# Reading out the sample states of a decoder step: one column moving past each state instead of the state moving past eight columns

## The chip, the core and the metric

The program runs on one core of a Trainium2 chip. A core has five engines that run at the same time and meet at semaphores: PE (TensorE, matmuls into PSUM), DVE (VectorE), ACT (ScalarE), POOL (GpSimd) and SP (SyncE, which here only issues DMAs). The metric is the device time of one execution in microseconds (us), lower is better.

## The reference

One inference step of a two-layer decoder for a prompt of 256 tokens and 8 samples of one token each. Both share all weights and run side by side as 264 columns. Layer 1 (the "odd" layer) has a Mamba-2 mixer with 32 heads of 64 channels in 4 groups, and a state of 128 numbers for each channel. For the samples its recurrence is one step from a given state:

```
    cb = jnp.einsum('bctgn,bcsgn->bctsg', cm, bm)
    dx = dt[..., None] * x
    y_diag = jnp.einsum('bctsgr,bcsgrp->bctgrp', cb[..., None] * decay, dx)
...
    states = jnp.einsum('bcsgn,bcsgrp->bcgrpn', bm, dstate[..., None] * dx)
...
        return dec[..., None, None] * carry + st, carry
```

For one token this is: new state = decay x old state + B (dt x), which is an output too (`s_ssd`), and y = C . new state, summed over the 128 state numbers n. Then y is gated, normalised and goes through the output projection. Everything is fp32.

## The kernel before

The odd mixer (`odd_mixer`) is one long loop over 41 tiles of the input projection (`k.linear(41, 8, "wio", ...)`): PE does the matmuls of tile m, then `use(m, p)` takes the result out, and from m = 9 on `slot(m - 9)` adds a slot's worth of other work behind it. The order on each engine is the order in which the code is written (`manual_schedule`); an engine never overtakes its own earlier instruction. Weight tiles come by DMA, issued by SP: some are used as they are (`wl`, line 128, plain fp32: two passes over 264 columns for a matmul), others come as `wr` and are split into `wh` by ACT (line 51) and `wl` by DVE or POOL (line 55), and then take three passes (lines 110 to 112).

The sample states are 32 units (g, b): 4 groups of 8 samples. A unit is a tile S of 128 state numbers (partitions) by 512 channels. `samples(want)` stands first in a slot (the "S" of `ORDER`), right behind the matmuls of the projection tile, and moves a few units on: `read` of those updated in an earlier slot, `update` (a matmul, line 1464, and a DVE pass, line 1465), `state_in` (DMA into one of 6 buffers S) and `decay` (POOL). `read(g, b, S)` issues the DMA that writes S out and multiplies it with C. In this kernel the small matrix `Cd[:, g, b*8:(b+1)*8]` (128 by 8, zero but for column b, made once by POOL at m = 10) is the stationary operand and S moves past it as 512 columns; the 8 units of a group add up in one PSUM tile `pys` (8 samples by 512 channels). The pool of `pys` has one buffer (one PSUM bank), so the next group's first write waits for whoever reads the last group's. Behind the eighth unit ACT copies `pys` to an SBUF tile `sd` (line 1477); the next call of `samples` first runs `turn_back` (line 1480): four PE transposes of `sd`, which bring channels back to the partitions, and a DVE copy into `ys`. So in three slots PE has four transposes between the projection tile and the next group's first read; the fourth `turn_back` has no read behind it.

In ACT's queue a slot begins with what `use` writes: `zt` twice (Tanh and copy of the projection tile, lines 1562 and 1563), then `act_queue` (waiting exponentials and SiLUs: lines 1365 to 1368 and 1313); the split of the next weight tile (line 51) stands ahead of these, since `linear` prepares weights while it issues the matmuls.

Of the kernel before, what the change touches and what calls it, by code (L numbers as in the profile page):

```python
# [7 lines left out]
F32 = mybir.dt.float32  # L8
# [4 lines left out]
AF = mybir.ActivationFunctionType  # L13
# [5 lines left out]
T = 264  # L19
NP = 256  # L20
NS = 8
# [1148 lines left out]
def odd_mixer(k, xh, xl, norm, mixed):  # L1170

    tc, nc, ins, outs = k.tc, k.nc, k.ins, k.outs
    V = nc.vector
    Act = nc.scalar.activation
    with ExitStack() as es:
        pool = es.enter_context(tc.tile_pool(name="od", bufs=1))
# [3 lines left out]
        gen = lambda: pg.tile([128, 512], F32, name="pgen")  # L1180
# [17 lines left out]
        xbc = pool.tile([128, 24, T], F32, name="xbc")  # L1198
# [9 lines left out]
        Bn = pool.tile([128, 2, 4, 128], F32, name="Bn")  # L1208
        cb = pool.tile([128, 2, 4, 128], F32, name="cb")
        sqa = pool.tile([128, T], F32, name="sqa")  # L1210
        Cd = pool.tile([128, 4, NS * NS], F32, name="Cd")
        ys = pool.tile([128, 16, NS], F32, name="ys")
        sqs = pool.tile([128, 16, NS], F32, name="sqs")
        ysw = pool.tile([128, 16, NS], F32, name="ysw")
# [180 lines left out]
        def sums(n):  # L1395
            s = st[n]
            py = gen()
            for i in range(2):
                R = slice(64 * i, 64 * i + 64)
                nc.tensor.matmul(py[R, 0:128], s["dx"][:, 0, R], s["seg"][:, i, 0], start=True, stop=True,  # L1400
                                 skip_group_check=True)
                nc.tensor.matmul(py[R, 128:256], s["dx"][:, 1, R], s["seg"][:, i, 1], start=True, stop=False,
                                 skip_group_check=True)
                nc.tensor.matmul(py[R, 128:256], s["St"][:, R], s["ea"][:, i], start=False, stop=True,
                                 skip_group_check=True)
            s["py"] = py

        def skip(n):
            y = xbc[:, n, 0:NP]
            V.scalar_tensor_tensor(y, y, dsk[:, 0, n:n + 1], st[n]["py"][:, 0:NP], op0=ALU.mult, op1=ALU.add)  # L1410
# [31 lines left out]
        def sample_x(g):  # L1442
            p = gen()
            for i in range(4):
                nc.tensor.transpose(p[:NS, ts(i, 128)], xbc[:, 4 * g + i, NP:T], k.ident)
            sd = pool.tile([NS, 512], F32, name="sd")
            V.tensor_tensor(sd.rearrange("b (h p) -> b h p", h=8), p[:NS].rearrange("b (h p) -> b h p", h=8),
                            snat[:, 8 * g:8 * g + 8, None].to_broadcast([NS, 8, 64]), op=ALU.mult)
            h = sdx[g] = sdr[:, g % 2]
            Act(h[:NS], sd, AF.Copy)  # L1450
            V.tensor_sub(h[32:], sd, h[:NS])

        def state_in(g, b):
            S = pool.tile([128, 512], F32, name="S", bufs=6)
            nc.sync.dma_start(S, ins["ssd0"][:, b, ts(g, 512)])
            return S

        def decay(g, b, S):
            nc.gpsimd.tensor_tensor(S.rearrange("n (h p) -> n h p", h=8), S.rearrange("n (h p) -> n h p", h=8),
                                    bc[:, 2 + b, 8 * g:8 * g + 8, None].to_broadcast([128, 8, 64]), op=ALU.mult)  # L1460

        def update(g, b, S):
            p = gen()
            nc.tensor.matmul(p, sel(NS, b), sdx[g], start=True, stop=True)
            V.scalar_tensor_tensor(S, p, xbc[:, 16 + g, NP + b:NP + b + 1], S, op0=ALU.mult, op1=ALU.add)

        pys = []

        def read(g, b, S):
            nc.sync.dma_start(outs["s_ssd"][:, b, ts(g, 512)], S)  # L1470
            if b == 0:
                pys.append(p1.tile([128, 512], F32, name="pys"))
            nc.tensor.matmul(pys[-1][:NS], Cd[:, g, b * NS:(b + 1) * NS], S, start=b == 0, stop=b == NS - 1,
                             skip_group_check=True)
            if b == NS - 1:
                y = pool.tile([NS, 512], F32, name="sd")
                Act(y, pys[-1][:NS], AF.Copy)
                turned.append((g, y))

        def turn_back(g, y):  # L1480
            p = gen()
            for i in range(4):
                nc.tensor.transpose(p[:, ts(i, NS)], y[:, ts(i, 128)], k.ident[:NS, :NS])
            V.tensor_copy(ys[:, 4 * g:4 * g + 4], p[:, 0:4 * NS].rearrange("p (i t) -> p i t", i=4))

        U = [(g, b) for g in range(4) for b in range(NS)]
        Ss, turned = {}, []
        at = [0, 0, 0, 0]

        def samples(want):  # L1490


            while turned:
                turn_back(*turned.pop(0))
            while at[3] < at[2]:
                read(*U[at[3]], Ss.pop(U[at[3]]))
                at[3] += 1
                if turned:
                    break
            while at[2] < want:  # L1500
                g, b = U[at[2]]
                assert at[1] > at[2]
                if b == 5 and g < 3:
                    sample_x(g + 1)
                update(g, b, Ss[g, b])
                at[2] += 1
            while at[0] < len(U) and at[0] < at[3] + 6:
                Ss[U[at[0]]] = state_in(*U[at[0]])
                at[0] += 1
            while at[1] < at[0] and at[1] < at[2] + 3:  # L1510
                decay(*U[at[1]], Ss[U[at[1]]])
                at[1] += 1


        start = {s: n for n, s in enumerate(START)}
        head, left = [], set(range(16))

        def slot(s):
            if s == 6:
                V.tensor_scalar(sdr[0:32], k.ones[0:32, 0:1, None].to_broadcast([32, 2, 512]), 0.0, None, op0=ALU.mult)  # L1520
                sample_x(0)
            for o in ORDER:
                if o == "S" and s > 5:
                    samples(SAMPLES[s - 6] if s - 6 < len(SAMPLES) else len(U))
                if o == "U" and s - 4 in start:
                    sums(start[s - 4])
                if o == "T" and s - 2 in start:
                    states(start[s - 2])
                if o == "W" and s - 2 in start:
                    weights(start[s - 2])  # L1530
                if o == "R" and s in start:
                    turns(start[s])
                if o == "K" and s - 4 in start:
                    skip(start[s - 4])
                    left.remove(start[s - 4])
            if s == LAST:
                assert at[3] == len(U) and not turned
                V.tensor_tensor(sqs, xbc[:, 0:16, NP:T], dsk[:, 0, :, None].to_broadcast([128, 16, NS]), op=ALU.mult)
                V.tensor_add(ys, ys, sqs)
                V.tensor_tensor(ysw, ys, dsk[:, 1, :, None].to_broadcast([128, 16, NS]), op=ALU.mult)  # L1540
            n = s - 16
            if 0 <= n < 16:
                assert n not in left
                if s > LAST:
                    sample_gate(0 if s == LAST + 1 else 2 * s - 47, min(16, 2 * s - 45))
                gate(n)
                if n > 0:
                    gated(n - 1)
                if n == 15:
                    gated(n)  # L1550

        def use(m, p):
            if m == 0:
                head.append(softplus(p))
                next(head[0])
                V.tensor_scalar(cw, cw, 0.5, None, op0=ALU.mult)
                return
            if m < 25:
                conv(m + 15 if m < 9 else m - 9, p)
            else:  # L1560
                z = pool.tile([128, 2, T], F32, name="zt", bufs=2)
                Act(z[:, 0], p[:, 0:T], AF.Tanh, scale=0.5)
                Act(z[:, 1], p[:, 0:T], AF.Copy)
                act_queue()
                finish_silus()
                V.scalar_tensor_tensor(z[:, 0], z[:, 0], 1.0, z[:, 1], op0=ALU.add, op1=ALU.mult)
                V.tensor_copy(szs[:, m - 25], z[:, 0, NP:T])
                st[m - 25]["z"] = z[:, 0]
            next(head[0], None)
            if m == 10:  # L1570
                groups()
                V.tensor_scalar(dsk[:, 1], dsk[:, 1], 0.5, None, op0=ALU.mult)
                y_parts.extend(pool.tile([128, 16, T], F32R, name=nm) for nm in ("yh", "yl"))
                nc.gpsimd.memset(Cd, 0.0)
                nc.gpsimd.tensor_copy(Cd[:, :, 0:NS * NS:NS + 1], xbc[:, 20:24, NP:T])
            if m >= 9:
                slot(m - 9)

# [185 lines left out]
```

## Time and profile before

| | |
|---|---|
| median of 3 runs | 2337.83 us (2336.58 to 2338.54) |
| the profiled execution | 2338.07 us, its span 2336.4 us |
| PE busy in the span | 2157.9 us (92%) |
| DVE, ACT, POOL busy | 1657.3, 945.1, 1008.6 us |
| mean granted TensorE clock | 0.967 of full speed |
| reads of the sample states | from 1189.2 to 1327.6 us of the span |

The span is the time from the first to the last instruction; 1.7 us lie around it. The granted clock has two levels, 1.0 (2.4 GHz) and 0.5 (1.2 GHz); the mean is over the span. An fp32 matmul is two PE records (passes) and two weight loads (PEld). A PE record's length includes time in which the array already works on the next one, so the distance between starts is what a pass costs.

### The profile page before, as it was taken

How to read it: one execution, taken by the hardware profiler on the slowest of the kernel's cores; microseconds unless marked ns; L12 is line 12 of the kernel's file. 1: busy time of each engine (PE TensorE's matmuls, PEld its weight loads, DVE VectorE, ACT ScalarE, POOL GpSimd, SP SyncE). 2: the span in 40 equal slices, each digit the busy share in tenths (PEclk: the TensorE clock that was granted, in tenths of full speed). 3: DMA queues.
4: the chain of work that ended last, by engine and by line, in shares of the span. 5: the costliest groups of instructions: out<-in, count | busy, mean ns of one | idle time of the engine just before them, and what ended most of it. 6: DMA issues, size and time to landing. Idle time of an engine off the chain costs nothing.

```text
span 2336.4 us, 44010 instructions
## 1 busy us (share of the span) xinstructions
PE 2157.9 (92%) x17885; PEld 2031.2 (87%) x17885; DVE 1657.3 (71%) x2862; ACT 945.1 (40%) x1390; POOL 1008.6 (43%) x695
## 2 busy tenths in 40 slices
PE   8699999789999779999999999999789999779998
PEld 6379999789999779999766799999789999779997
DVE  8945699998743995445888755789998653995444
ACT  2424454224444224444543444444224444223443
POOL 6714444564534453222445334444554543553221
PEclk9799999899999889999999999999899999989999
DMA  5025554434775334553346545555434775334553
GB/s 178 26 93 176 178 181 163 136 114 149 264 244 178 109 109 154 185 177 133 132 145 220 172 142 165 187 172 170 137 109 145 260 236 187 120 105 149 183 172 106
DMA packets 111659, 371.56 MB, mean 159 GB/s; under 512 B 13865, under 2 KB 17857, under 8 KB 111456
## 3 DMA queue, kind: packets, MB, share of 16 engines
q1 hardware_dynamic: 104400, 347.73, 44.6%
q0 software_dynamic: 5728, 19.95, 2.5%
q8 instruction: 140, 2.29, 0.4%
q10 hardware_dynamic: 1328, 1.07, 0.1%
q14 instruction: 63, 0.52, 0.1%
HBM read 356.52 MB, written 12.18 MB: 158 GB/s over the span
## 4 chain that ended last, share of the span: by engine, by line
PE 55%; DVE 37%; DMA 3%; issue 2%; ACT 2%; POOL 1%; SPq 0%; ACTq 0%; DVEq 0%; POOLq 0%
PE Y L110 7%; PE Y L111 7%; PE Y L112 7%; PE pmm L110 7%; PE pmm L111 7%; PE pmm L112 7%; DVE ohG L470 7%; DVE ohG L453 4%; PE pmm L128 4%; DVE ohB L453 4%; DVE wl L55 3%; DVE tkt L209 3%; DVE S L443 3%; DVE tkt L211 2%; DVE al L488 2%
## 5 line engine op out<-in xcount | busy, mean ns | idle before, releaser
L55 POOL TENSOR_TENSOR wl<-wr,wh 128x1024 fp32r<-128x1024 f32 x303 | 759.9, 2511 | 998.4 <-ACT wh L51 937.1
L51 ACT ACTIVATE wh<-wr 128x1024 fp32r<-128x1024 f32 x579 | 610.2, 1055 | 645.1 <-PE pmm L111 144.2
L110 PE MATMUL pmm<-xh,wh 128*128 128x256 f32 (+1 forms) x2456 | 709.9, 289 | 1.9 <-ACT S L421 0.8
L112 PE MATMUL pmm<-xh,wl 128*128 128x256 f32 (+1 forms) x2456 | 697.0, 284 | 9.0 <-DVE wl L55 6.0
L111 PE MATMUL pmm<-xl,wh 128*128 128x256 f32 (+1 forms) x2456 | 698.6, 284 | 1.4 <-DVE xl L647 1.0
L110 PE MATMUL Y<-ah,wh 128*128 128x256 f32 x2048 | 592.6, 289 | 0.0
L55 DVE TENSOR_TENSOR wl<-wr,wh 128x1024 fp32r<-128x1024 f32 x276 | 364.5, 1321 | 321.2 <-ACT wh L51 320.4
L111 PE MATMUL Y<-al,wh 128*128 128x256 f32 x2048 | 586.8, 287 | 3.0 <-DVE al L488 2.9
L112 PE MATMUL Y<-ah,wl 128*128 128x256 f32 x2048 | 585.7, 286 | 0.0
L112 PEld LDWEIGHTS pmm<-xh,wl 128*128 128x128 f32 x2456 | 470.1, 191 | 10.6 <-DVE wl L55 7.2
L110 PEld LDWEIGHTS pmm<-xh,wh 128*128 128x128 f32 x2456 | 470.3, 191 | 5.0 <-ACT S L421 1.0
L111 PEld LDWEIGHTS pmm<-xl,wh 128*128 128x128 f32 x2456 | 471.2, 192 | 2.7 <-DVE xl L647 2.2
L111 PEld LDWEIGHTS Y<-al,wh 128*128 128x128 f32 x2048 | 400.3, 195 | 4.1 <-DVE al L488 4.0
L110 PEld LDWEIGHTS Y<-ah,wh 128*128 128x128 f32 x2048 | 400.4, 196 | 0.1
L112 PEld LDWEIGHTS Y<-ah,wl 128*128 128x128 f32 x2048 | 399.9, 195 | 0.0
L488 DVE TENSOR_TENSOR al<-S,ah 128x512 fp32r<-128x512 f32 x128 | 108.3, 848 | 157.1 <-ACT ah L486 157.1
L470 DVE TENSOR_TENSOR ohG<-ohG,gT 128x1024 f16<-128x1024 f16 x128 | 181.4, 1417 | 2.3
L486 ACT ACTIVATE ah<-S 128x512 fp32r<-128x512 f32 x128 | 80.5, 629 | 240.8 <-PE Y L112 236.8
L434 PE MATMUL pgen<-ohG,ohB 128*128 128x64 f16 x2048 | 87.2, 199 | 96.2 <-DVE ohG L470 82.9
L421 ACT ACTIVATE S<-pmm 128x512 f32<-128x512 f32 x128 | 76.3, 596 | 231.3 <-PE pmm L112 230.9
L434 PEld LDWEIGHTS <-ohB 128*128 128x128 f16 x2048 | 72.0, 101 | 107.9 <-DVE ohG L470 76.8
L128 PE MATMUL pmm<-x,wl 128*128 128x264 f32 x512 | 124.9, 401 | 7.9 <-DMA wl<-in_wie 6.6
(446 smaller groups left out, 2362.2 us busy)
## 6 DMA issues: line engine op xcount, KB each, us to landing
wr<-in_ut SPq DMA_DIRECT2D x256, 512.0 KB, 3.4
wr<-in_v SPq DMA_DIRECT2D x256, 512.0 KB, 3.4
wr<-in_wq SPq DMA_DIRECT2D x32, 512.0 KB, 3.5
wl<-in_wio SPq DMA_DIRECT2D x22, 512.0 KB, 3.6
wr<-in_wio SPq DMA_DIRECT2D x19, 512.0 KB, 4.8
S<-in_ssd SPq DMA_DIRECT2D x32, 256.0 KB, 2.7
out_s_ssd<-S SPq DMA_DIRECT2D x32, 256.0 KB, 3.0
wr<-in_woo SPq DMA_DIRECT2D x16, 512.0 KB, 4.0
```

What stands on the lines that cost most here:

```text
L51: k.nc.scalar.activation(hi, w, AF.Copy)
L55: eng.tensor_tensor(lo, w, hi, op=ALU.subtract)
L110: mm(out, wh, xh, start=first, stop=False, skip_group_check=True)
L111: mm(out, wh, xl, start=False, stop=False, skip_group_check=True)
L112: mm(out, wl, xh, start=False, stop=last, skip_group_check=True)
L128: self.nc.tensor.matmul(p[:, :T], wl[:, ts(i, 128)], x[:, kt], start=kt == 0, stop=kt == nk - 1, skip_group_check=True)
L421: nc.scalar.activation(S[s][:, e2:e2 + 2], p.rearrange("p (e t) -> p e t", e=2), AF.Gelu_apprx_tanh)
L434: nc.tensor.matmul(p[:, t * n:(t + 1) * n], B[:, 8 * h + t], AG[:, 8 * h + t, g], start=g == 0 and t == 0, stop=g == 1 and t == 7, skip_gr ...
L453: V.tensor_tensor(cols(out), iotah[:, i:i + n].rearrange("p (o a b) -> p o a b", o=1, b=2) .to_broadcast([128, nt, n // 2, 2]), spread(iT[ ...
L470: V.tensor_tensor(cols(AG[:, :, g]), cols(AG[:, :, 0]), spread(gT[:, g, tt], n), op=ALU.mult)
L486: nc.scalar.activation(ah, v, AF.Copy)
L488: V.tensor_sub(al, v, ah)
```

## The change

The roles in `read` are exchanged. Now the state is stationary: four matmuls for a unit, each with 128 channels of S (128 by 128) as the stationary operand and one column of C, `xbc[:, 20 + g, NP + b]`, moving past. The result has channels on the partitions: column i*8 + b of `pys`. Nothing is accumulated over units, `Cd` is not needed, and there is no `turn_back`. In its place `take_out(g)` is one ACT copy of 128 by 32 from `pys` into `ys`. It stands where `turn_back` stood, at the start of the next call of `samples`, while ACT's old copy (line 1477) stood behind the group's last read.

```
-        Cd = pool.tile([128, 4, NS * NS], F32, name="Cd")
...
-            nc.tensor.matmul(pys[-1][:NS], Cd[:, g, b * NS:(b + 1) * NS], S, start=b == 0, stop=b == NS - 1,
-                             skip_group_check=True)
+            for i in range(4):
+                nc.tensor.matmul(pys[-1][:, i * NS + b:i * NS + b + 1], S[:, ts(i, 128)], xbc[:, 20 + g, NP + b:NP + b + 1],
+                                 start=True, stop=True, skip_group_check=True)
             if b == NS - 1:
-                y = pool.tile([NS, 512], F32, name="sd")
-                Act(y, pys[-1][:NS], AF.Copy)
-                turned.append((g, y))
-
-        def turn_back(g, y):
-            p = gen()
-            for i in range(4):
-                nc.tensor.transpose(p[:, ts(i, NS)], y[:, ts(i, 128)], k.ident[:NS, :NS])
-            V.tensor_copy(ys[:, 4 * g:4 * g + 4], p[:, 0:4 * NS].rearrange("p (i t) -> p i t", i=4))
+                done.append(g)
+
+        def take_out(g):
+            Act(ys[:, 4 * g:4 * g + 4], pys[g][:, 0:4 * NS].rearrange("p (i t) -> p i t", i=4), AF.Copy)
...
-            while turned:
-                turn_back(*turned.pop(0))
+            while done:
+                take_out(done.pop(0))
             while at[3] < at[2]:
                 read(*U[at[3]], Ss.pop(U[at[3]]))
                 at[3] += 1
-                if turned:
+                if done:
                     break
...
-                nc.gpsimd.memset(Cd, 0.0)
-                nc.gpsimd.tensor_copy(Cd[:, :, 0:NS * NS:NS + 1], xbc[:, 20:24, NP:T])
```

On PE, this is the slot in which group 1 is begun, before: the last matmuls of the projection tile, the four transposes (they wait for ACT, the copy into `sd`), the reads of two units, the next updates. The square brackets name the engines whose semaphores an instruction waits for.

```order
L128 MATMUL pmm<-x,wl 128x264 x7
L1483 MATMUL pgen<-ident,sd 128x8 [waits DVE_49,Activation_49]
L1483 MATMUL pgen<-ident,sd 128x8 x3
L1473 MATMUL pys<-S,Cd 8x512 [waits Pool_49]
L1473 MATMUL pys<-S,Cd 8x512 [waits DVE_49]
L1464 MATMUL pgen<-sdr,identr 128x512
```

The same place now:

```order
L128 MATMUL pmm<-x,wl 128x264 x7
L1473 MATMUL pys<-xbc,S 128x1 [waits PE_49,Activation_49,Pool_49]
L1473 MATMUL pys<-xbc,S 128x1 x3
L1473 MATMUL pys<-xbc,S 128x1 [waits DVE_49]
L1473 MATMUL pys<-xbc,S 128x1 x3
L1463 MATMUL pgen<-sdr,identr 128x512 x2
```

The transposes are gone, a unit is four matmuls of one column, and the group's first read itself waits for ACT: for `take_out` of the group before, which frees the one `pys` buffer.

On ACT, from the last slot of group 0 into the slot in which group 1 is begun, before: the copy into `sd`, a state copy, the split of a weight tile (it waits for a DMA), and the next slot's work.

```order
L1477 ACTIVATE sd<-pys 8x512 [waits PE_49]
L1379 ACTIVATE St<-pgen 128x128 [waits PE_49]
L51 ACTIVATE wh<-wr 128x1024 [waits DMAHW0_49]
L1562 ACTIVATE zt<-pmm 128x264 [waits PE_49]
L1563 ACTIVATE zt<-pmm 128x264
L1367 ACTIVATE ea<-pgen 128x256 [waits DVE_49]
L1368 ACTIVATE seg<-seg 128x512
L1313 ACTIVATE xbc<-cy 128x256
```

The same place now:

```order
L1378 ACTIVATE St<-pgen 128x128 [waits PE_49]
L51 ACTIVATE wh<-wr 128x1024 [waits DMAHW0_49]
L1557 ACTIVATE zt<-pmm 128x264 [waits PE_49]
L1558 ACTIVATE zt<-pmm 128x264
L1366 ACTIVATE ea<-pgen 128x256 [waits DVE_49]
L1367 ACTIVATE seg<-seg 128x512
L1312 ACTIVATE xbc<-cy 128x256
L1479 ACTIVATE ys<-pys 128x32
```

ACT's reading of `pys` has moved from the head of this list to its end, behind the weight split and the slot's own work. At the start of group 2 it stands like this:

```order
L51 ACTIVATE wh<-wr 128x1024 [waits DMAHW4_49]
L1557 ACTIVATE zt<-pmm 128x264 [waits PE_49]
L1558 ACTIVATE zt<-pmm 128x264
L1479 ACTIVATE ys<-pys 128x32
L1378 ACTIVATE St<-pgen 128x128 [waits PE_49]
```

It has moved behind the split and the two `zt` there, and the same holds at the start of group 3.

## Rows read from the trace of the kernel before

**Rows 1.** Stretch 1236 to 1345: length, PE, PEld, DVE, ACT, POOL busy, clock, DMA.

```profile
1236.00:1345.00 109.00, 108.74 (x580) 72.56 (x579) 86.79 (x179) 43.42 (x112) 43.74 (x52) 1.00 0.58 189
```

**Rows 2.** Who PE waited for in the same stretch: us, times, longest.

```profile
PE pgen L1344 <- DVE ys L1484: 0.3, 1, 0.3
```

**Rows 3.** Chain that ended last, 1235 to 1336: time, us, piece.

```profile
1236.60 0.34 PE pgen L1483 x4
1236.94 1.81 PE pys L1473 x4
...
1268.59 2.67 PE pys L1473 x6
...
1272.81 0.19 DVE ys L1484
...
1326.62 0.96 PE pys L1473 x2
1327.57 0.64 PE pgen L1375 x4
```

**Rows 4.** Costliest groups, shapes apart, 1180 to 1340: the read passes.

```profile
L1473 PE MATMUL pys<-S,Cd 128*8 128x512 f32 x64 | 30.5, 593 | 1.8 <-DVE S L1465 1.7
```

**Rows 5.** Weight loads in order of time near 997 (another stage).

```profile
996.46 1.88 PEld L530 LDWEIGHTS pgen<-rep,x 128*128 128x128 f32 x16
998.26 0.19 PEld L110 LDWEIGHTS Y<-ah,wh 128*128 128x128 f32 x1
```

**Rows 6.** PE in order of time at three starts of a group: start, us.

```profile
1235.76 0.83 PE L128 MATMUL pmm<-x,wl 128*128 128x264 f32 x3
1236.53 0.41 PE L1483 MATMUL pgen<-ident,sd 8*128 8x8 f32 x4
1236.87 1.88 PE L1473 MATMUL pys<-S,Cd 128*8 128x512 f32 x4
...
1268.18 0.41 PE L1483 MATMUL pgen<-ident,sd 8*128 8x8 f32 x4
...
1299.20 0.41 PE L1483 MATMUL pgen<-ident,sd 8*128 8x8 f32 x4
```

**Rows 7.** ACT in order of time, 1226 to 1245; brackets: idle before, ended by.

```profile
1231.16 0.59 ACT L1477 ACTIVATE sd<-pys 8x512 f32<-8x512 f32 x1 [0.43 <-PE pys L1473]
...
1237.40 1.06 ACT L51 ACTIVATE wh<-wr 128x1024 fp32r<-128x1024 f32 x1 [4.89 <-DMA wr<-in_wio]
...
1238.64 0.38 ACT L1563 ACTIVATE zt<-pmm 128x264 f32<-128x264 f32 x1
1238.91 0.39 ACT L1367 ACTIVATE ea<-pgen 128x256 f32<-128x256 f32 x1
...
1239.69 0.42 ACT L1313 ACTIVATE xbc<-cy 128x256 f32<-128x256 f32 x1
...
1244.83 0.23 ACT L1313 ACTIVATE xbc<-sy 128x32 f32<-128x32 f32 x1
```

**Rows 8.** ACT in order of time at the starts of groups 2 and 3.

```profile
1270.03 1.06 ACT L51 ACTIVATE wh<-wr 128x1024 fp32r<-128x1024 f32 x1 [6.82 <-DMA wr<-in_wio]
...
1271.27 0.38 ACT L1563 ACTIVATE zt<-pmm 128x264 f32<-128x264 f32 x1
...
1299.91 0.38 ACT L1563 ACTIVATE zt<-pmm 128x264 f32<-128x264 f32 x1
```

**Rows 9.** SP's DMA issues in order of time, 1230 to 1240.

```profile
1230.71 0.96 SPq L1455 DMA_DIRECT2D S<-in_ssd  x2
1231.72 0.48 SPq L49 DMA_DIRECT2D wr<-in_wio  x1
```

**Rows 10.** Stretches in which PE stood, each followed by one at half clock.

```profile
456.17:460.09 3.92, 0.00 (x0) 0.00 (x1) 3.88 (x5) 0.54 (x1) 2.70 (x1) 1.00 0.40 134
461.33:464.73 3.40, 3.40 (x18) 3.40 (x17) 3.06 (x7) 0.00 (x0) 0.00 (x0) 0.50 0.27 99
1738.76:1742.67 3.91, 0.00 (x0) 0.00 (x0) 3.88 (x5) 0.54 (x1) 2.69 (x1) 0.83 0.40 134
1742.67:1748.14 5.47, 5.46 (x37) 5.47 (x38) 4.30 (x8) 0.00 (x0) 0.00 (x0) 0.50 0.31 96
```

**Rows 11.** PE in order of time, 1174 to 1183, half clock until 1181.5.

```profile
1175.20 0.79 PE L1344 MATMUL pgen<-acr,identr 64*128 64x256 f32 x2 [1.91 <-DVE Sf L1385]
1175.92 6.58 PE L128 MATMUL pmm<-x,wl 128*128 128x264 f32 x16
```

More of the change, by code (lines that the diff above doesn't have):

```diff
@@ L1472, in read @@
                 pys.append(p1.tile([128, 512], F32, name="pys"))
-            nc.tensor.matmul(pys[-1][:NS], Cd[:, g, b * NS:(b + 1) * NS], S, start=b == 0, stop=b == NS - 1,
-                             skip_group_check=True)
+            for i in range(4):
+                nc.tensor.matmul(pys[-1][:, i * NS + b:i * NS + b + 1], S[:, ts(i, 128)], xbc[:, 20 + g, NP + b:NP + b + 1],
+                                 start=True, stop=True, skip_group_check=True)
             if b == NS - 1:
-                y = pool.tile([NS, 512], F32, name="sd")
-                Act(y, pys[-1][:NS], AF.Copy)
-                turned.append((g, y))
-        def turn_back(g, y):
-            p = gen()
-            for i in range(4):
-                nc.tensor.transpose(p[:, ts(i, NS)], y[:, ts(i, 128)], k.ident[:NS, :NS])
-            V.tensor_copy(ys[:, 4 * g:4 * g + 4], p[:, 0:4 * NS].rearrange("p (i t) -> p i t", i=4))
+                done.append(g)
+        def take_out(g):
+            Act(ys[:, 4 * g:4 * g + 4], pys[g][:, 0:4 * NS].rearrange("p (i t) -> p i t", i=4), AF.Copy)
         U = [(g, b) for g in range(4) for b in range(NS)]
-        Ss, turned = {}, []
+        Ss, done = {}, []
         at = [0, 0, 0, 0]
         def samples(want):
-            while turned:
-                turn_back(*turned.pop(0))
+            while done:
+                take_out(done.pop(0))
             while at[3] < at[2]:
@@ L1536, in slot @@
             if s == LAST:
-                assert at[3] == len(U) and not turned
+                assert at[3] == len(U) and not done
                 V.tensor_tensor(sqs, xbc[:, 0:16, NP:T], dsk[:, 0, :, None].to_broadcast([128, 16, NS]), op=ALU.mult)
```

## The prediction

> **What bounds the kernel now.** I looked first at the stretch of the odd mixer in which the sample states are read, by busy time. From 1236 to 1345 PE is busy for 108.74 of 109 us at full clock, DVE for 86.79, ACT and POOL for 43 each [rows 1]. The waits of that stretch confirm it: PE waited for another engine once, 0.3 us, at a tile that a turn-back had held [rows 2]. The chain of work that ended last runs through PE there, piece after piece, the reads and the turn-backs among them [rows 3]. So whatever PE gains or loses in these slots moves the end by as much, and PE has no slack to swallow a wait. Whether it gets one was then read from ACT's and SP's queues in order of time [rows 7 to 9].
>
> **The change part by part.**
>
> *The passes of a read.* Before, a unit is two passes of 512 columns (64 passes for 32 units [rows 4]): three units take 2.67 us in the chain and two take 1.81 [rows 3], so one costs 0.86, and 0.10 is left over once for each run of units. After, a unit is four fp32 matmuls, which is eight loads of 128 by 128 with one column behind each. The nearest row is a matmul of the same stationary shape with 8 columns: 16 loads start within 998.26 - 996.46 = 1.80 us, 0.112 each, and the short passes hide behind the loads [rows 5]. Eight are 0.90, so a unit costs 0.04 more, 32 units +1.3 us. From below, the four turn-back transposes take 0.34 together [rows 3], under 0.09 each, and 256 such steps would be 6 us less; but their stationary operand has 8 partitions and a transpose is one pass, so I take the 0.112. From above, a load's own record is 0.19 us long (the single load of [rows 5]); if loads didn't overlap, 256 x 0.08 = +20 us. The row of 16 speaks against it.
>
> The Trainium skill, "TensorE: Matmul & The Clock Gate", section "LDWEIGHTS (loading the stationary operand)", counts a load by its columns over 1.2 GHz, 0.107 us for 128. By that figure a unit would come to an estimated 0.85 us, no more than before, and the 1.3 us would vanish. The row has 0.112, and I keep it.
>
> *The pause ahead of a read.* Three passes of the projection take 0.83 us: two steps of 0.22 and a record of 0.39. The third starts at 1236.20 and the next instruction at 1236.53, 0.33 later and not 0.22 [rows 6]: 0.10 is lost where the stationary operand changes from 128 by 128 to a smaller shape, and 16 loads of 128 by 128 behind other such matmuls lose nothing [rows 5]. The new read is 128 by 128. The code has 17 runs of reads, all behind a projection tile; 14 have no turn-back ahead of them: -1.4.
>
> *The turn-back.* At the three starts of a group the first read could begin at 1236.20 + 0.22 = 1236.42 instead of 1236.87 [rows 6]: 3 x -0.45; the fourth turn-back saves its 0.34, and the wait of 0.19 for its DVE copy goes [rows 3]: together -1.9. ACT's copy into `sd` and POOL's making of `Cd` lie off the path.
>
> *Leaving a run.* Three runs go over to L1375, 128 by 128 too. Before, a run of one unit takes 0.96, 0.10 over the 0.86, and the four passes of L1375 take 0.64 and not 4 x 0.11 plus one pause of 0.10 [rows 3]: 0.20 each, -0.6. The other 14 go over to smaller shapes, so the pause stays; only it now follows a pass of one column, whose load is not followed by another: between 0 and -0.11 each. I take -0.08, -1.1.
>
> Together PE does -3.7 us of work (-2.6 if the last item is nothing).
>
> *The new wait.* PE's first read of groups 1, 2 and 3 waits for `take_out`, and this stands in ACT's queue behind what the slot gives ACT first. Before, ACT had emptied `pys` by 1231.16 + 0.59, 5 us ahead of the turn-back at 1236.53 [rows 6, 7]. Group 1: ACT gets its weight tile at 1237.40, after 4.89 us of waiting for a DMA, then runs the split, two `zt`, `ea`, `seg` and the SiLU at 1239.69 [rows 7]. The copy would start one such step later (0.27, as between `zt` at 1238.64 and `ea` at 1238.91), take 0.23 as the 128 by 32 ACT does, and PE starts after a load (0.11) and some 0.07 for the signal, my guess: 1239.69 + 0.68 = 1240.37 instead of 1236.42, a wait of 3.95. Group 2: the second `zt` at 1271.27 + 0.27 + 0.23 + 0.18 = 1271.95 against 1268.18 - 0.11 = 1268.07, 3.9 [rows 6, 8]. Group 3: 1299.91 + 0.68 = 1300.59 against 1299.09, 1.5 [rows 6, 8]. Sum +9.3. Behind the waiting read in PE's queue stand all updates, sums and projection tiles of the slot, and ACT, DVE and SP wait for those, so nothing later catches up. The DMA is SP's issue at 1231.72 behind two loads of S, which wait for PE's reads and their stores [rows 9]; so it moves with PE and comes no earlier relative to it. Nobody but DVE's sum in the last slot waits for the fourth copy.
>
> *The clock.* PE will stand for nearly 4 us twice. In the two stretches shown PE stood for 3.92 and 3.91 us, and behind each the granted clock is 0.50, 1.2 GHz, for 3.40 and 5.47 us of PE's work [rows 10]; in the mixer itself a wait of 1.91 was followed by passes some 0.41 apart instead of 0.22 [rows 11]. Half of 4.4 us lost, twice: +4.4. The 1.5 us wait I count as free of it. From below 0, from above 2 x 3.4 (a stretch as in [rows 11] of 6.8 us).
>
> The Trainium skill, "TensorE: Matmul & The Clock Gate", Part 1, says that the throttled state is the default and activity lifts it; by that rule both waits cost clock, and the trace agrees with its 0.50 behind both stretches. Without the rule the sum would be the 4.4 us less of the second rival below.
>
> Sum: -3.7 + 9.3 + 4.4 = +10.0 on the profiled execution's 2338.07, 2348.1. The median of the runs is 0.24 below that execution, so **2348 us**, 0.4% slower. A difference under 0.2%, 4.7 us, can hardly be told from none here.
>
> **The rivals.**
>
> *1. Waits and clock as above*: 2348 (2344.5 to 2352).
>
> *2. Waits, but the clock holds*: 2337.83 - 3.7 + 9.3 = 2343.4, just slower. The short stand in [rows 11] and both of [rows 10] speak against it.
>
> *3. ACT is early* (the other side): the wait is only the two `zt` and the copy, because the weight tile has landed by then. Group 3 is nearly such a case with 1.5 us [rows 8]; three of those are +4.5, no clock is lost, and the time is 2338.6, no change. It decides if the DMA lands more than 2 us earlier relative to PE's projection tile in both long slots; against it, the tile is issued behind loads that follow PE [rows 9].
>
> *4. No wait that matters*: if the copy found ACT idle and `pys` free, only the -3.7 stand: 2334.1, no measurable change, faster at best. That needs ACT to reach the copy ahead of its weight split, and its queue says otherwise.
>
> *5. Loads that don't overlap*: +20 on the first: 2368. Only the row of single loads speaks for it.
>
> **How the numbers follow.** First case 0.60, second 0.15, third 0.11, fourth 0.06, fifth 0.03, the rest (waits as forecast, but part of them given back by DMA, or more clock lost) 0.05 around them. The forecast is the first. The range reaches down into the third case at 2340, and up to 2353, where two long stretches at half clock and no gain on leaving a run (1.1) end: about 0.8 lies between. Slower by over 0.2% (above 2342.5) are the first, the fifth and most of the second: 0.80. Within 0.2%: the third, most of the fourth and what is left of the second: 0.16. Faster: 0.04.
>
> **What the changed profile would show.** Right: the first read of groups 1, 2 and 3 waits for ACT's `ys` line, near 4, 4 and 1.5 us, and PE is busy for clearly less of this stretch; half clock behind the first two; the loads of a unit 0.112 apart; no 0.10 between a projection tile and a read; no DVE `ys` in the chain. Wrong: `ys` on ACT ending before PE's projection tile does, loads 0.19 apart, or full clock through the whole stretch. The forecast fails most easily by the landing time of the weight tiles, which I take from one execution.

## The result and the profile after

The changed kernel takes 2361.78 us (median of 4 runs, 2359.51 to 2366.48), the kernel before on the same chip 2337.20 (4 runs, 2334.88 to 2338.54): a ratio of 1.0109, 95% interval 1.0091 to 1.0126. It is slower, as forecast, but by 24.6 us instead of 10, and beyond the upper end of the range.

The profiled execution after took 2361.34 us, 23.3 more than the one before. To see where, I cut out the stage of the sample states in both: from the first update matmul of a state to the first pass of the output projection. The rows are of the view by windows, one of the kernel before and one of the kernel after; the columns are those of [rows 1].

```profile
1182.44:1342.03 159.59, 157.42 (x849) 106.01 (x849) 132.14 (x268) 64.94 (x172) 68.21 (x95) 1.00 0.55 184
```

```profile
1183.46:1363.36 179.90, 172.48 (x1025) 145.16 (x1025) 132.26 (x264) 63.15 (x172) 68.04 (x95) 0.89 0.51 164
```

The stage is 20.3 us longer, which is all but 3.0 of the difference. PE stands for 179.90 - 172.48 = 7.4 us instead of 2.2, so 5.3 are waits, and it is *busy* for 15.1 us more. The granted clock, 1.00 before, is 0.89: at two levels of 1.0 and 0.5 that is (1 - 0.89) x 2 x 179.9, some 40 us at half clock (the clock is rounded to 0.01, which is up to 2 us here).

The waits in the stage after, as the view of PE's waits lists them:

```profile
PE pys L1473 <- issue: 3.9, 1, 3.9
PE pys L1473 <- ACT ys L1479: 1.6, 1, 1.6
PE pys L1473 <- POOL ea L1391: 1.6, 1, 1.6
PE pys L1473 <- DVE S L1464: 0.3, 1, 0.3
```

The first three are the group starts, 7.1 us together. Two are put down to something else than ACT, but ACT's queue shows that its copy ended last. At the starts of the three groups ACT in order of time is (start, length, instruction, idle before it and what ended that):

```profile
1240.74 1.06 ACT L51 ACTIVATE wh<-wr 128x1024 fp32r<-128x1024 f32 x1 [5.05 <-DMA wr<-in_wio]
...
1243.03 0.42 ACT L1312 ACTIVATE xbc<-cy 128x256 f32<-128x256 f32 x1
1243.33 0.20 ACT L1479 ACTIVATE ys<-pys 128x32 f32<-128x32 f32 x1
...
1280.84 1.06 ACT L51 ACTIVATE wh<-wr 128x1024 fp32r<-128x1024 f32 x1 [5.73 <-DMA wr<-in_wio]
...
1282.34 0.20 ACT L1479 ACTIVATE ys<-pys 128x32 f32<-128x32 f32 x1
...
1318.51 0.20 ACT L1479 ACTIVATE ys<-pys 128x32 f32<-128x32 f32 x1
```

And PE in order of time, same columns:

```profile
1223.46 0.29 PE L112 MATMUL pmm<-xh,wl 128*128 128x264 f32 x1
1223.58 1.84 PE L1473 MATMUL pys<-xbc,S 128*128 128x1 f32 x16
1225.35 0.95 PE L1463 MATMUL pgen<-sdr,identr 40*128 40x512 f32 x3
...
1243.64 3.31 PE L1473 MATMUL pys<-xbc,S 128*128 128x1 f32 x16 [3.86 <-issue]
...
1282.59 3.25 PE L1473 MATMUL pys<-xbc,S 128*128 128x1 f32 x24 [1.65 <-ACT ys L1479]
...
1318.80 3.70 PE L1473 MATMUL pys<-xbc,S 128*128 128x1 f32 x32 [1.59 <-POOL ea L1391]
```

Where the rows of before have four transposes at a group's start [rows 6], there is now a read, and PE starts it 0.05 to 0.11 us after `ys` (L1479) has run (1243.33 + 0.20 against 1243.64). The two units at 1223.58 take 1225.35 - 1223.58 = 1.77 up to the next instruction, 0.89 a unit, at full clock. From the first start to the last end such 16 passes take 1.84 there and 3.31 at 1243.64, behind the wait.

The half clock isn't all behind waits. Three neighbouring windows of the kernel after, same columns as above:

```profile
1220.00:1226.80 6.80, 6.80 (x41) 6.33 (x40) 5.19 (x13) 2.85 (x7) 1.19 (x2) 0.75 0.34 116
1226.80:1230.21 3.41, 3.41 (x20) 3.00 (x19) 3.37 (x7) 0.00 (x0) 1.73 (x2) 0.51 0.84 293
1230.21:1235.00 4.79, 4.79 (x40) 4.54 (x40) 3.14 (x8) 1.32 (x4) 3.43 (x9) 1.00 0.32 102
```

PE is busy in every microsecond of these 15, and this is ahead of the first group wait, which ends at 1243.64. Yet the first window is at half clock for half of its length (0.75), the second, which begins 1.5 us behind the read of 1223.58 to 1225.35, for all of it (0.51), and the third not at all. This is what the experiments had to explain.

### The profile page after: what moved, and what is told of

It reads as the page before. It is cut to its first block, busy times and chain, and to the rows that moved or that the text cites. A ratio compares the mean times of both kernels' runs of the same rounds, so it can differ in the third digit from the quotient of the medians.

```text
span 2359.7 us, 44360 instructions
## 1 busy us (share of the span) xinstructions
PE 2181.0 (92%) x18061; PEld 2075.2 (88%) x18061; DVE 1662.4 (70%) x2858; ACT 943.2 (40%) x1390; POOL 1008.5 (43%) x693
## 4 chain that ended last, share of the span: by engine, by line
PE 57%; DVE 34%; DMA 4%; ACT 2%; issue 2%; POOL 1%; SPq 0%; ACTq 0%; DVEq 0%; POOLq 0%
PE pmm L110 8%; PE pmm L111 8%; PE pmm L112 8%; PE Y L110 7%; PE Y L111 7%; PE Y L112 7%; DVE ohG L470 7%; DVE ohG L453 4%; DVE ohB L453 4%; PE pmm L128 3%; DVE wl L55 3%; DVE S L443 3%; DVE tkt L209 2%; DVE al L488 2%; DVE tkt L211 1%
## 5 line engine op out<-in xcount | busy, mean ns | idle before, releaser
L112 PE MATMUL pmm<-xh,wl 128*128 128x256 f32 (+1 forms) x2456 | 700.1, 285 | 9.7 <-DVE wl L55 6.7
L112 PE MATMUL Y<-ah,wl 128*128 128x256 f32 x2048 | 585.6, 286 | 0.0
L112 PEld LDWEIGHTS pmm<-xh,wl 128*128 128x128 f32 x2456 | 473.3, 193 | 11.1 <-DVE wl L55 7.7
L112 PEld LDWEIGHTS Y<-ah,wl 128*128 128x128 f32 x2048 | 399.7, 195 | 0.1
L128 PE MATMUL pmm<-x,wl 128*128 128x264 f32 x512 | 132.5, 419 | 7.4 <-DMA wl<-in_wie 6.7
```

Source lines behind the costliest of these rows:

```text
L112: mm(out, wl, xh, start=False, stop=last, skip_group_check=True)
L128: self.nc.tensor.matmul(p[:, :T], wl[:, ts(i, 128)], x[:, kt], start=kt == 0, stop=kt == nk - 1, skip_group_check=True)
```

## The experiments

Three theories. A: reads whose passes carry few columns let the clock fall by themselves, though PE is busy; the waits add theirs. B: the clock falls only because PE stood; without the waits it holds. C: of the reads, only the form with a single column lets it fall. All runs are compared with the kernel before on the same chip: a median of 2335.88 us (15 runs) for the first four, 2334.39 (10 runs) for the last two. "Stage" is the stretch defined above.

**One column, copy early.** `take_out` is called right behind a group's last read, where the kernel before had its copy into `sd`.

```
             if b == NS - 1:
+                take_out(g)
                 done.append(g)
...
-            while done:
-                take_out(done.pop(0))
+            done.clear()
```

> The changed kernel with one thing moved: ACT's copy out of the PSUM tile stands right behind a group's last read, as in the kernel before, and not at the start of the next slot. So no first read waits (7.1 us of waits in the changed kernel: 3.9, 1.6 and 1.6). Theory A (a read of one-column passes by itself lets the clock fall): the waits and the 10 us stretch at half clock behind the long one go, but stretches behind reads stay, some 20 to 30 us of them between 1180 and 1340; time 2337 - 3.7 + 10 to 15, about 2344 to 2349. Theory B (the clock falls because PE stood, and what follows is its aftermath): no half clock in the reads any more, time about 2333.5.

2347.25 us (4 runs, 2341.35 to 2351.67), ratio 1.0039 (1.0024 to 1.0054). The stage, PE's waits in it, and five windows of it (the profiled execution, 2351.67, is the slowest of the four):

```profile
1183.40:1354.06 170.66, 168.73 (x1026) 142.40 (x1025) 133.83 (x265) 63.39 (x172) 69.70 (x97) 0.90 0.53 172
...
1266.80:1270.20 3.40, 3.40 (x17) 2.75 (x18) 3.33 (x7) 0.00 (x0) 1.13 (x2) 0.50 0.86 220
1277.10:1280.50 3.40, 3.40 (x11) 2.57 (x11) 3.20 (x7) 0.98 (x3) 2.97 (x4) 0.50 0.95 278
1294.10:1297.50 3.40, 3.40 (x18) 2.64 (x17) 3.25 (x6) 1.18 (x3) 1.13 (x2) 0.50 0.85 256
1311.20:1318.00 6.80, 6.80 (x32) 5.92 (x29) 2.75 (x7) 0.00 (x0) 1.82 (x3) 0.50 0.61 211
1321.40:1324.80 3.40, 3.40 (x13) 2.21 (x11) 2.31 (x7) 1.44 (x3) 0.73 (x1) 0.50 0.20 77
```

```profile
PE pys L1473 <- DVE S L1464: 1.7, 1, 1.7
```

The time is where A had it (2344 to 2349). The group waits are gone; the one that is left stood in the kernel before too [rows 4]. The clock is 0.90 all the same, about 34 us at half clock, and in the five windows shown (20.4 us) PE doesn't idle for a moment. B falls. A sixth stretch of 10.2 us (1222.4 to 1232.6) begins while PE stands in the wait of 1.7, and can't be put down to the reads alone: the kernel before has the same wait and a clock of 1.00, but with nothing changed except ACT's copy (the fourth run below) 3.4 us at half clock follow that wait. So some 24 of the 34 us have no wait ahead of them that could explain them.

**120 columns, copy late.** The change as it was made, but behind each load 120 columns of `xbc` move past instead of one. The wanted column is the first; the other results are overwritten or never read. POOL clears a margin of `xbc` once.

```
-        xbc = pool.tile([128, 24, T], F32, name="xbc")
+        WIDE = 120
+        xf = pool.tile([128, 24 * T + 128], F32, name="xbc")
+        xbc = xf[:, 0:24 * T].rearrange("p (i t) -> p i t", t=T)
...
+                o, c = i * (WIDE + 7) + b, (20 + g) * T + NP + b
+                nc.tensor.matmul(pys[-1][:, o:o + WIDE], S[:, ts(i, 128)], xf[:, c:c + WIDE],
```

> The changed kernel with 120 columns moving past each state block instead of one (the wanted column of C first, 119 further columns of the same tile behind it; of each unit's 120 result columns the first is kept, the rest is overwritten or never read). Such a pass needs about 0.10 us, less than the 0.112 us of the weight load beside it, so PE's time for a read should not change; ACT's copy stays late. Theory A: the half clock behind reads goes, the three waits stay, and behind the 3.9 us wait one stretch at half clock may stay: 2337 - 3.7 + 7 + 2 to 5, about 2342 to 2346. Theory B: nothing changes against the changed kernel, about 2361.

2348.24 us (4 runs, 2347.40 to 2352.81), ratio 1.0057 (1.0041 to 1.0072). Windows (the stage, and the stretch around the first group wait), then PE's three group starts in order of time:

```profile
1179.05:1352.02 172.97, 161.66 (x1026) 135.46 (x1025) 131.81 (x264) 63.22 (x172) 68.50 (x95) 0.96 0.52 170
...
1236.30:1246.50 10.20, 8.89 (x35) 7.32 (x36) 4.07 (x8) 1.21 (x5) 2.09 (x2) 0.50 0.46 156
```

```profile
1237.61 3.74 PE L1476 MATMUL pys<-xbc,S 128*128 128x120 f32 x16 [4.04 <-issue]
...
1276.68 1.16 PE L1476 MATMUL pys<-xbc,S 128*128 128x120 f32 x6 [3.54 <-ACT ys L1482]
...
1310.22 3.80 PE L1476 MATMUL pys<-xbc,S 128*128 128x120 f32 x32 [1.55 <-issue]
```

The waits are 4.04, 3.54 and 1.55, those of the forecast. Of the 40 us at half clock some 14 are left, 10.2 of them around the first of the long waits; A had 2 to 5 us of lost time for them, and the run is 2 us above A's range.

**120 columns, copy early.** Both edits.

> Both edits: 120 columns move past each state block, and ACT's copy stands right behind a group's last read. Theory A: no waits, no half clock between 1180 and 1340, and only PE's saving of 3.7 us stays: about 2333.5, faster than the kernel before by some 0.15%. Theory B gives the same here; if the loads themselves (not the columns) let the clock fall, it falls here too and the time is about 2345.

2335.27 us (11 runs, 2332.26 to 2339.52), ratio 1.0002 (0.9993 to 1.0011): the time of the kernel before. The stage, and the chain that ended last from 1225 to 1235 (time, length, piece):

```profile
1178.52:1335.12 156.60, 154.80 (x1026) 130.69 (x1025) 132.84 (x265) 63.55 (x172) 70.44 (x97) 1.00 0.57 188
```

```profile
1225.08 1.78 PE pys L1476 x16
...
1228.58 3.76 PE pmm L128 x16
1232.33 1.78 PE pys L1476 x16
```

Full clock throughout and no group wait. In PE's work only the columns differ from the first experiment, the loads are the same, and the stage is 14.1 us shorter. So it isn't the loads as such that let the clock fall. The profiled execution is the fastest of the 11; but no run here is as slow as the fastest of the first experiment (2339.52 against 2341.35). In the same view of the first experiment, runs of one to four units at full clock stand as:

```profile
1248.59 1.68 PE pys L1473 x16
...
1273.73 2.57 PE pys L1473 x24
...
1300.64 0.78 PE pys L1473 x8
...
1306.51 3.46 PE pys L1473 x32
```

A further unit costs 0.89 or 0.90 there, and a run of two is 0.10 shorter than with 120 columns. So the columns pass while the next load runs, and only those of a run's last pass cost time. The stage is also 3.0 us shorter than before, but the median over the runs doesn't show it; 3.0 us are 0.13%, just outside the interval. The version that takes both troubles away is level with the kernel before, not better.

**The kernel before, copy late.** The other half alone: 512 columns and turn-back as before, but ACT's copy into `sd` is written at the start of `turn_back`, in the next slot.

```
-                y = pool.tile([NS, 512], F32, name="sd")
-                Act(y, pys[-1][:NS], AF.Copy)
-                turned.append((g, y))
+                turned.append((g, pys[-1]))
...
+            y = pool.tile([NS, 512], F32, name="sd")
+            Act(y, py[:NS], AF.Copy)
```

> The kernel before with one thing moved: ACT's copy of the PSUM tile into SBUF stands at the start of the next slot, just ahead of the turn-back, so that the four transposes wait for it as the changed kernel's first read does; the reads stay 512 columns wide. Theory A: three waits of about 4, 3.5 and 2 us (the copy is 0.59 us instead of 0.20), and half clock behind the long ones alone, 3 to 10 us of it, so 2337 + 9 + 2 to 5, about 2348 to 2351. Theory B (waits set off most of the half clock of the changed kernel, 41 us in all): about 2360 or more.

2351.91 us (4 runs, 2350.39 to 2353.33), ratio 1.0069 (1.0053 to 1.0084). The stage, and PE's waits in it:

```profile
1177.34:1356.68 179.34, 167.04 (x849) 109.68 (x849) 131.63 (x269) 64.46 (x172) 70.44 (x97) 0.94 0.50 164
```

```profile
PE pgen L1483 <- ACT sd L1480: 10.0, 4, 3.9
PE pys L1473 <- DVE S L1465: 2.3, 3, 1.7
```

Where the copy stands in ACT's queue is enough, without any change to the reads, for 10.0 us of waits and, with passes of 512 columns, 20 to 22 us at half clock, where A had 3 to 10; the time is just above A's range. Besides 10.2 us around the first wait there are three stretches of 3.4 us, one of them ahead of every group wait, 1.9 us behind the old wait for S that ends at 1217.89:

```profile
1219.80:1223.20 3.40, 3.40 (x18) 2.84 (x19) 2.48 (x5) 0.97 (x3) 1.60 (x2) 0.50 0.81 280
```

In that place the code is that of the kernel before, which kept its clock. So a stand of 1.7 us can cost clock with wide reads too, in one execution and not in another.

**8 and 32 columns, copy early.** The third kernel with `WIDE` at 8 and at 32.

> As the run with 120 columns and the early copy, but with 8 columns moving past each state block, so that PE's time for loads is the same 0.112 us each and only the columns differ. Theory A (the clock falls because so few columns pass in a read): most of the half clock of the one-column run with the early copy stays (34 us between 1180 and 1340), say 15 to 34 us, and the time lies between that run and the 120-column run, 2341 to 2348. Rival C (it is the form of a single column alone that counts as no work): no half clock in the reads, about 2335.

> The same with 32 columns. Theory A: less half clock than with 8 columns, 0 to 15 us, and 2335 to 2342. Rival C: the same as with 8 and with 120 columns, about 2335.

8 columns: 2352.12 us (5 runs, 2339.17 to 2354.12), ratio 1.0080 (1.0063 to 1.0097). 32 columns: 2346.86 (7 runs, 2337.79 to 2350.01), 1.0048 (1.0030 to 1.0066). Both are slower than either theory had it (A: 2341 to 2348 and 2335 to 2342). The two stages, 8 columns first, are of executions of 2339.17 and 2340.30, below their medians, so they show less of the loss than most runs had:

```profile
1180.10:1342.89 162.79, 161.17 (x1026) 136.52 (x1025) 133.65 (x264) 63.51 (x172) 68.66 (x95) 0.95 0.56 181
```

```profile
1178.75:1343.24 164.49, 161.88 (x1026) 136.70 (x1025) 133.57 (x265) 63.50 (x172) 69.55 (x97) 0.95 0.55 179
```

Both keep 16 to 17 us at half clock without a group wait. Of these, 6.8 us (8 columns) and 3.4 us (32) begin 0.9 and 1.7 us behind the end of the old wait for S. The other 10 and 13 us stand behind reads with PE busy throughout, as in these rows, 8 columns first:

```profile
1288.40:1291.80 3.40, 3.40 (x19) 3.07 (x19) 3.33 (x7) 0.22 (x1) 1.95 (x3) 0.50 0.90 244
```

```profile
1303.20:1309.90 6.70, 6.70 (x33) 5.81 (x32) 4.40 (x9) 0.00 (x0) 2.48 (x3) 0.50 0.66 231
```

So C falls: it isn't the form with one column. A holds as far as 32 columns lose clock and 120 don't. That the loss shrinks steadily with the columns isn't shown: 8 columns have a higher median than one, the two profiles are alike, and the runs of either kernel spread over 12 to 15 us.

## Why the prediction was wrong

All stages side by side, from their rows (idle is length less PE busy; half clock is (1 - clock) x 2 x length, good to some 2 us):

| kernel | stage, us | PE busy | PE idle | half clock |
|---|---|---|---|---|
| before | 159.6 | 157.4 | 2.2 | 0 |
| after: 1 column, late | 179.9 | 172.5 | 7.4 | 40 |
| 1 column, early | 170.7 | 168.7 | 1.9 | 34 |
| 120 columns, late | 173.0 | 161.7 | 11.3 | 14 |
| 120 columns, early | 156.6 | 154.8 | 1.8 | 0 |
| before, copy late | 179.3 | 167.0 | 12.3 | 22 |
| 8 columns, early | 162.8 | 161.2 | 1.6 | 16 |
| 32 columns, early | 164.5 | 161.9 | 2.6 | 16 |

The 120 columns with the early copy have the new read without half clock or group waits, so they split the 20.3 us: PE's work 154.8 - 157.4 = -2.6, clock 172.5 - 154.8 = +17.7, idle 7.4 - 2.2 = +5.3. (With one column PE's work would be some 1.7 less, by the estimate below, and the clock's part that much more.)

- **The clock is the step that failed.** It counted half clock only behind the two long waits: "+4.4", at most 6.8. It was +17.7, because reads of one column bring the clock down with PE busy: 13.9 us of busy time (168.7 - 154.8) are lost with the group waits gone, for 34 us at half clock, of which some 10 begin in the old wait for S. The prediction weighed that an engine that stands loses its clock, and took for granted that one that is busy keeps it; no rival had it otherwise. The kernel after has these stretches at half clock beside the 3.41 us shown above:

```profile
1216.60:1223.40 6.80, 6.80 (x28) 5.93 (x28) 6.04 (x10) 1.50 (x4) 2.12 (x4) 0.50 0.44 154
1243.90:1254.10 10.20, 10.20 (x39) 8.28 (x40) 2.94 (x7) 0.00 (x0) 2.09 (x2) 0.50 0.46 157
1267.80:1271.20 3.40, 3.40 (x15) 3.17 (x15) 3.40 (x10) 0.66 (x2) 1.74 (x2) 0.50 0.93 234
1284.90:1291.70 6.80, 6.80 (x21) 5.06 (x21) 4.53 (x12) 0.98 (x3) 4.25 (x6) 0.50 0.81 264
1305.40:1308.70 3.30, 3.30 (x19) 2.75 (x18) 3.23 (x7) 0.56 (x2) 1.56 (x2) 0.50 0.86 246
1322.50:1329.30 6.80, 6.80 (x30) 5.26 (x30) 3.28 (x7) 0.00 (x0) 2.77 (x3) 0.50 0.75 255
```

  The three that begin 0.3, 2.3 and 3.7 us behind a group wait's end (1243.64, 1282.59, 1318.80) hold 23.8 us, where the forecast had 8.9 behind two waits and counted the third as free; the other four hold 16.9, where it had none. Where the reads carry 120 columns the step holds better: 161.7 - 154.8 = 6.9 us, just above its upper bound, and the idle time is +9.1 (11.3 - 2.2). That kernel is 12.4 us above the kernel before (2348.24 - 2335.88) where 10 were forecast: the forecast fits a kernel whose reads leave the clock alone.
- **The new wait** was right in place and cause, and for groups 1 and 3 in size: 3.86 and 1.59 against 3.95 and 1.5. Group 2 has 1.65 instead of 3.9. The forecast said that the weight tile's DMA moves with PE; part of it doesn't. From the start of the read one slot earlier to the start of ACT's split of that tile are 10.03 us before (1260.00 to 1270.03), 10.07 with 120 columns and a late copy (1264.85 to 1274.92), and 8.09 in the kernel after (1272.75 to 1280.84), where PE had just been late at half clock (1267.8 to 1271.2); with 120 columns that wait is 3.54. That the lateness is the reason fits these times, but no run changes it by itself. The waits of the stage are +5.3 and not +9.3, since besides group 2's the old wait for S of 1.7 [rows 4] is gone, in a slot that PE reached late at half clock; the one of 0.3 is another, ahead of the stage's third run of reads. So the waits gave back 4 us of what the clock took. From the end of ACT's copy to PE's read 0.05 to 0.11 us pass, less than the 0.18 that the prediction took for a load and its guess at the signal.
- **The passes of a read** were right: a further unit costs 0.89 or 0.90 at full clock, the forecast's 0.90, and rival 5, loads apart, is out. The figure of the Trainium skill that the prediction weighed ("TensorE: Matmul & The Clock Gate", section "LDWEIGHTS (loading the stationary operand)") gave an estimated 0.85; the measurement decides for the row.
- **Pause and leaving a run**: L112 at 1223.46 is followed by the read 0.12 later, the step of such passes, so the pause ahead is gone. On leaving, a run of 8 passes takes 0.78 and not 8 x 0.112 = 0.90, so 0.11 is saved, the upper bound of what the forecast allowed (0.08 taken). In the chain a run of two is 1.68 against 1.81 [rows 3].
- **The sum of PE's work** can be measured only with 120 columns, where the last pass of each of 17 runs costs its 0.10 again: -3.0 us with the idle time, against -3.7 for one column. With one column it would be about 3.0 + 17 x 0.10 = 4.7, an estimate, since no run has one column at full clock throughout.
- **Rivals 2 to 4**: the clock doesn't hold and the waits are there. Rival 3, an early ACT, is out for group 1, but group 2's wait is of its kind: the tile came 1.9 us earlier relative to PE (10.03 against 8.09).
- **The range**: its upper end of 2353 doesn't follow from the two terms named for it. They add 2.4 (6.8 - 4.4) and 1.1 to 2347.8, which gives 2351.3.

What stays open: why some reads bring the clock down and others don't (behind the one at 1248.59 in the first experiment it stayed at full), and from how many columns on none does (between 32 and 120 here); and why a wait is followed by half clock in one execution and not in another. The 3.0 us outside the stage were not followed up. The Trainium skill, "TensorE: Matmul & The Clock Gate", Part 4 (PE-mode transpose), says that work of one kind, transposes, doesn't count for the clock as other work does. No run here shows that for transposes; reads that are nearly all weight load behave in that way.

## What to carry to other kernels

When stationary and moving operand are exchanged so that PE does mostly weight loads, read the granted clock of the stretch and not only its busy share: PE can be busy throughout at half speed (20.4 us of the first experiment). Letting more columns move past than are needed, as far as they hide behind the next load, kept the clock here with 120 and not with 32. And count where the instruction that empties a single-buffered PSUM tile stands in its engine's queue: a place one slot later cost 10 us of waits with no other edit, and half clock behind them.

## What was unexpected of the hardware

- PE lost its clock while busy for 100% of a window: 0.50 in the 20.4 us listed of the first experiment.
- 120 columns behind each load cost 0.10 us more than one column for a whole run of two units, 16 passes (1.78 and 1.68).
- Half clock cost nearly what it says: 0.39 to 0.50 us of busy time for each us of it, by the six stages of the table that have any (PE busy against the stage of its kind at full clock: 120 columns early, or before). That it is less than a half isn't shown, with half clock good to some 2 us a stage.
- A stand of PE of 1.7 us was followed by half clock in one execution (0.50 from 1219.8 to 1223.2 of the kernel before with the late copy) and not in another (1.00 through the whole stage of the kernel before).
